# Multiplications and additions on the samples' states scheduled ahead of other work in a hybrid decoder step

## The chip, the cores and the metric

The kernel runs on one core of a Trainium2 chip. The metric is the device time of one execution in microseconds. Its engines are TensorE (matrix products; PE in the profile, PEld its loads of weights), VectorE (DVE), ScalarE (ACT), GpSimd (POOL) and SyncE (SP), which only issues DMAs here. Each engine works through its own list of instructions in a fixed order, and waits on semaphores for the others.

## What is computed

One step of a one-layer decoder trunk, for a prompt of 256 tokens and for 8 samples with 8 new tokens each (320 tokens in all, model width 2048). Cut to what matters:

```python
h = rms_norm(x)
u, v, z, xBC, dt = split(h @ W_in)            # 2048, 2048, 2048, 3072 and 32 columns
xBC = silu(causal_depthwise_conv(xBC))        # 4 taps
y, state = ssd_scan(x, dt, a, B, C, state)    # 32 heads of 64, 4 groups, state of 128
mix = concat(chunk_mlp(u, v), rms_norm(y * silu(z)))
x = x + rms_norm(mix @ W_out)
x = x + rms_norm(conv_ffn(rms_norm(x)))       # 2048 -> 2 x 5632 -> 2048
```

The scan has for each sample and head a state of 64 x 128 numbers that comes in and goes out. Over the 8 new tokens of a sample it becomes

```python
new_state = state * exp(total decay) + sum over tokens of (decayed x) * B
```

The change is about this line for the samples: the multiplication, and the addition of the sum.

## The kernel before

**Products.** All matrices are in float32. `slab` (L109 to L126) loads 128 x 1024 weights with SyncE (`wraw`, L115), makes their high part on ScalarE (`whi`, L118) and their low part on VectorE (`wlo`, L120). `accumulate` (L127 to L131) makes three matmuls of a product: high by high (L129), high by low (L130), low by high (L131). There are three buffers of each kind. A load is issued when its buffer comes free; SyncE's list is in a fixed order, so what is behind a load that waits also waits.

**Stages.** `project` computes columns of W_in slab by slab, `chunk_out` computes four row blocks of W_out and adds each result to a sum in SBUF (L217, VectorE). The groups of the scan are computed beside them: `ssd(g)` is a generator, and after each slab `tick` runs it to its next `yield`. So the scan's instructions are issued between the large products, for groups 0 to 3 in the order of this list:

```python
chunk_out(w_out, 3, ...); heads_out(0); heads_in_next(2)
chunk_out(w_out, 4, ...); heads_out(1); heads_in_next(3)
chunk_out(w_out, 5, ...); heads_out(2); heads_out(3)
```

`heads_in` projects x, B and C for a group, with the convolution on VectorE (`cv`, L388, three per block), ScalarE and GpSimd (small copies L378, L379, L390, L391). `heads_out` projects z, multiplies the scan's result with silu(z) (L963), sums squares (ScalarE L281, VectorE L282, TensorE's `tsum` L263) for the norm.

**A group's states.** The 8 samples are taken in four pairs i = 0 to 3, with two tiles `st` of 128 x 512 each, six buffers in all. SyncE loads them (L743), TensorE multiplies them with C (`yo_ps`, L817), ScalarE picks the samples' B (`bm`, L822), and GpSimd multiplies them by the decay in `shrunk` (L825 to L828, the operation is recorded at L827). A step later `grown` (L830 to L835) makes two matmuls `up_ps` (L833) and adds them to the tiles with VectorE (L834). ScalarE then issues the stores (L839). `up_ps` takes its PSUM bank from the pool `ms`, of four banks, that most small products of the kernel share (`misc`); a bank is given back when its reader has run. State loads of the next pairs or groups wait for stores to land, since they use the same six buffers.

**The scan's products.** For each two heads SyncE loads sums of decays (`cs`, L750), VectorE (L895) and ScalarE (L888, L897) make their exponentials, VectorE masks them (L899), TensorE multiplies (`y_ps`, L910). `yo_to_xdt` (L845) puts the product with the old states beside x.

**The order of the work.** A scheduler orders each engine's list when the program is compiled. What is issued inside `tc.high_priority(offset=...)` is taken ahead of other work that is ready; `first()` is this with an offset of 200000, and slabs use 100000. Additions of `chunk_out` (L217), the reading of the convolution's input and what belongs to a norm are inside `first()` already; the convolution (L388) is not.

Of the kernel before, what the change touches and what calls it, by code (L numbers as in the profile page):

```python
# [13 lines left out]
ALU = mybir.AluOpType  # L14
# [3 lines left out]
P = 128  # L18
# [16 lines left out]
def hybrid_step(  # L35
# [10 lines left out]
    act, dve, pool, pe, sp = nc.scalar, nc.vector, nc.gpsimd, nc.tensor, nc.sync  # L46
# [10 lines left out]
    def misc(name):  # L57
        return ms.tile([P, 512], F32, tag="ms", name=name)
# [6 lines left out]
    with tc.high_priority(offset=300000):  # L65
        dve.memset(ones, 1.0)

        ps = misc("early")
# [35 lines left out]
    def first():  # L104

        return tc.high_priority(offset=200000)
# [151 lines left out]
    def token_sums(*sqs):  # L258

        ps = misc("tsum")  # L260
        for c, o in enumerate((0, P, NT - P)):
            for i, sq in enumerate(sqs):
                ins = pe.matmul(ps[:, c:c + 1], sq[:, o:o + P], ones[:, 0:1], start=i == 0, stop=i == len(sqs) - 1).ins  # L263
        sums_ins.append(ins)
        return ps[:, 0:3]
# [98 lines left out]
    with ExitStack() as mctx:  # L364
        op = mctx.enter_context(tc.tile_pool(name="op", bufs=1))
# [43 lines left out]
        tote = op.tile([P, NH, NB], F32, name="tote")  # L409
# [296 lines left out]
        with tc.tile_pool(name="sd", bufs=1) as sd:  # L706
# [7 lines left out]
            for c in range(4):  # L714
                ps = misc("bt_ps")
# [11 lines left out]
            def by_head(ap):  # L727
                return ap.rearrange("p (h d) -> p h d", d=64)
# [4 lines left out]
            def ssd(g):  # L733

                xs = x_of[g]
                h0 = 8 * g
# [25 lines left out]
                for c in range(4):  # L762
                    ps = misc("xt_ps")
# [6 lines left out]
                    i = c - 2  # L770
# [7 lines left out]
                ps = misc("cb_ps")  # L778
# [3 lines left out]
                for r in range(2):  # L782
# [3 lines left out]
                                  in0=ps[:, :NP].rearrange("p (c t) -> p c t", c=2),  # L786
                                  in1=upper.unsqueeze(1).to_broadcast([P, 2, P]), op=ALU.mult)
# [11 lines left out]
                for hb in range(2):  # L799
                    dve.tensor_tensor(out=cms[:, 4 * hb:4 * hb + 4], in0=cmask[:, 4 * hb:4 * hb + 4],  # L800
                                      in1=cT[:, g, NP + 32 * hb:NP + 32 * hb + 32].unsqueeze(1).to_broadcast([P, 4, 32]),
                                      op=ALU.mult)
                yield

                ps = misc("s1_ps")
# [17 lines left out]
                    return bm  # L823

                def shrunk(i, st):  # L825
                    for h in range(2):
                        pool.tensor_tensor(out=by_head(st[h]), in0=by_head(st[h]),  # L827
                                           in1=tote[:, h0:h0 + 8, 4 * h + i:4 * h + i + 1].to_broadcast([P, 8, 64]), op=ALU.mult)  # L828

                def grown(st, bm):  # L830
                    for h in range(2):
                        ps = misc("up_ps")
                        made = pe.matmul(ps, bm[:, h], xsp[:, h], start=True, stop=True)  # L833
                        dve.tensor_tensor(out=st[h], in0=st[h], in1=ps, op=ALU.add)  # L834
                    return made.ins  # L835

                def store_state(i, st, by=act):
# [12 lines left out]
                def begin(i):  # L850
                    with_c(i, sts[i])
                    bms[i] = picked(i)
                    shrunk(i, sts[i])

                def end(i, by=act):
                    made = grown(sts[i], bms.pop(i))
                    store_state(i, sts[i], by)
                    return made
# [63 lines left out]
                for j in range(5):  # L922
                    for i in range(2):
                        if j < 4:
                            decays(2 * j + i)
                        if j and i == 0:
# [5 lines left out]
                                   in1=dec[:, 2, h0:h0 + 8].unsqueeze(2).to_broadcast([P, 8, 64]), op=ALU.mult)  # L932
# [78 lines left out]
            with first():  # L1011
# [4 lines left out]
                with tc.issue_after(sums_ins[-1]):  # L1016
                    ps = token_sums(*one)
# [37 lines left out]
    with tc.tile_pool(name="fp", bufs=1) as fp:  # L1055
# [113 lines left out]
        with tc.issue_after(made):  # L1169
            ps = token_sums(*one)  # L1170
# [109 lines left out]
```

## Time and profile before

| | |
|---|---|
| median of 3 runs | 1798.79 us (1796.71 to 1799.12) |
| profiled execution, whole | 1800.87 us |
| its span | 1799.2 us |
| VectorE's work from 460 to 560 us | 86.02 of 100 us |
| VectorE's work from 560 to 650 us | 77.55 of 90 us |
| TensorE's work from 560 to 650 us | 88.94 of 90 us |
| additions to states (L834) | 32, 0.68 us each |
| multiplications of states (L827) | 32, 1.05 to 2.62 us each, median 1.22 |

The span runs from the first to the last instruction of the trace; the profiled execution's own time is 1.67 us longer. In a row of the timeline stand the start, the duration, the engine, the line, the operation, the tiles and their shapes and, in brackets, how long the engine stood idle before it and who ended that. SPq and ACTq are DMAs issued by SyncE and ScalarE. In a row of the windows view stand the stretch, its length, then the busy time of TensorE, its weight loads, VectorE, ScalarE and GpSimd with the number of instructions, TensorE's granted clock as a share of full speed, the DMA share and GB/s.

### The profile page before, as it was taken

What the parts mean: (1) busy time and instruction counts of PE and PEld (TensorE: products, weight loads), DVE (VectorE), ACT (ScalarE), POOL (GpSimd) and SP (SyncE); (2) the same over time, 40 slices, a digit from 0 to 9 for tenths busy, and PEclk for the clock granted to TensorE, in tenths of its full rate; (3) what the DMA queues carried; (4) which work ended last, traced back from release to release, by engine and by line L of the source; (5) the groups of instructions that cost most, each with busy time, mean ns of one, the idle gap of its engine ahead of it and who ended that gap; (6) DMA issues with size and microseconds to landing.
All of it is one profiled execution on the core that took longest, in us unless ns stands there. A gap on an engine that the chain in (4) does not pass through costs nothing.

```text
span 1799.2 us, 31167 instructions
## 1 busy us (share of the span) xinstructions
PE 1776.3 (99%) x12200; PEld 1741.7 (97%) x12200; DVE 1190.1 (66%) x2048; ACT 795.4 (44%) x1105; POOL 295.4 (16%) x619
## 2 busy tenths in 40 slices
PE   9999999999999999999999999999999999999998
PEld 8999999999889899999999999999999999999997
DVE  5458664556987969776875474747566565656575
ACT  6444454334545446445554433333434343433335
POOL 3102200000431313104331010111101020101004
PEclk9999999999999999999999999999999999999999
DMA  8646544455566574654554555455545554454542
GB/s 276 194 141 195 159 143 152 153 153 177 180 193 192 167 234 147 178 169 146 174 149 151 155 152 151 148 154 153 153 145 154 152 156 145 153 152 153 151 150 102
DMA packets 222226, 292.56 MB, mean 163 GB/s; under 512 B 16672, under 2 KB 150656, under 8 KB 221888
## 3 DMA queue, kind: packets, MB, share of 16 engines
q1 hardware_dynamic: 209392, 268.12, 49.3%
q10 hardware_dynamic: 10304, 14.82, 2.3%
q0 software_dynamic: 2384, 7.64, 1.4%
q8 instruction: 96, 1.57, 0.4%
q14 instruction: 50, 0.41, 0.1%
HBM read 275.71 MB, written 14.82 MB: 161 GB/s over the span
## 4 chain that ended last, share of the span: by engine, by line
PE 92%; DVE 4%; DMA 2%; issue 1%; ACT 1%; POOL 0%; ACTq 0%; DVEq 0%; POOLq 0%
PE ps L129 20%; PE ps L131 19%; PE ps L130 19%; PE pd L129 10%; PE pd L131 10%; PE pd L130 10%; DMA wraw<-in_w_in 1%; DVE wlo L120 1%; PE y_ps L910 1%; PE yo_ps L817 0%; PE up_ps L833 0%; PE sg L670 0%; ACT whi L118 0%; PE tsum L263 0%; PE vt_ps L582 0%
## 5 line engine op out<-in xcount | busy, mean ns | idle before, releaser
L120 DVE TENSOR_TENSOR wlo<-wraw,whi 128x1024 fp32r<-128x1024 f32 (+1 forms) x474 | 587.6, 1240 | 440.0 <-ACT whi L118 438.2
L118 ACT CAST whi<-wraw 128x1024 fp32r<-128x1024 f32 (+1 forms) x475 | 494.7, 1042 | 717.1 <-PE ps L130 414.8
L129 PE MATMUL ps<-h_hi,whi 128*128 128x320 f32 x2524 | 783.5, 311 | 4.0 <-ACT h_hi L346 2.1
L131 PE MATMUL ps<-h_hi,wlo 128*128 128x320 f32 x2524 | 781.4, 310 | 2.1 <-DVE wlo L120 1.9
L130 PE MATMUL ps<-h_lo,whi 128*128 128x320 f32 x2524 | 780.8, 309 | 0.0
L129 PEld LDWEIGHTS ps<-h_hi,whi 128*128 128x128 f32 x2524 | 475.6, 189 | 7.9 <-issue 2.7
L131 PEld LDWEIGHTS ps<-h_hi,wlo 128*128 128x128 f32 x2524 | 475.4, 188 | 4.1 <-DVE wlo L120 3.5
L130 PEld LDWEIGHTS ps<-h_lo,whi 128*128 128x128 f32 x2524 | 475.6, 188 | 0.7 <-DVE h_lo L546 0.2
L129 PE MATMUL pd<-fhi,whi 128*128 128x320 f32 x704 | 217.2, 309 | 0.0
L131 PE MATMUL pd<-fhi,wlo 128*128 128x320 f32 x704 | 217.2, 309 | 0.0
L130 PE MATMUL pd<-flo,whi 128*128 128x320 f32 x704 | 217.2, 308 | 0.0
L129 PE MATMUL pd<-ohi,whi 128*128 128x320 f32 x448 | 139.6, 312 | 0.0
L131 PE MATMUL pd<-ohi,wlo 128*128 128x320 f32 x448 | 138.4, 309 | 0.0
L130 PE MATMUL pd<-olo,whi 128*128 128x320 f32 x448 | 138.3, 309 | 0.0
L130 PEld LDWEIGHTS pd<-flo,whi 128*128 128x128 f32 x704 | 132.2, 188 | 0.0
L129 PEld LDWEIGHTS pd<-fhi,whi 128*128 128x128 f32 x704 | 132.2, 188 | 0.0
L131 PEld LDWEIGHTS pd<-fhi,wlo 128*128 128x128 f32 x704 | 132.2, 188 | 0.0
L1091 POOL COPY ptf<-pad 128x2 f32<-128x2 f32 x88 | 21.0, 238 | 621.1 <-DVE pad L1079 620.4
L217 DVE TENSOR_TENSOR acc_ffn<-acc_ffn,pd 128x320 f32<-128x320 f32 x160 | 77.6, 485 | 37.9 <-PE pd L131 36.4
L129 PEld LDWEIGHTS pd<-ohi,whi 128*128 128x128 f32 x448 | 84.1, 188 | 1.4 <-issue 0.6
L131 PEld LDWEIGHTS pd<-ohi,wlo 128*128 128x128 f32 x448 | 84.1, 188 | 0.5 <-issue 0.4
L130 PEld LDWEIGHTS pd<-olo,whi 128*128 128x128 f32 x448 | 84.2, 188 | 0.2
(301 smaller groups left out, 1592.3 us busy)
## 6 DMA issues: line engine op xcount, KB each, us to landing
wraw<-in_ffn_w_up SPq DMA_DIRECT2D x176, 512.0 KB, 3.7
wraw<-in_w_in SPq DMA_DIRECT2D x144, 512.0 KB, 3.7
wraw<-in_ffn_w_down SPq DMA_DIRECT2D x88, 512.0 KB, 3.5
wraw<-in_w_out SPq DMA_DIRECT2D x64, 512.0 KB, 3.5
st<-in_state_ssm SPq DMA_DIRECT2D x32, 256.0 KB, 4.5
out_ssm_state_sample<-st ACTq DMA_DIRECT2D x30, 256.0 KB, 4.6
cs<-dacs_d SPq DMA_DIRECT2D x16, 320.0 KB, 4.3
xr<-in_xT SPq DMA_DIRECT2D x4, 640.0 KB, 4.0
```

The costliest lines, as they stand in the source:

```text
L118: act.copy(hi[:, o], raw[:, o])
L120: dve.tensor_tensor(out=lo[:, :m], in0=raw[:, :m], in1=hi[:, :m].bitcast(F32), op=ALU.subtract)
L129: pe.matmul(ps, whi, xhi, start=first, stop=False)
L130: pe.matmul(ps, whi, xlo, start=False, stop=False)
L131: return pe.matmul(ps, wlo, xhi, start=False, stop=last).ins
L217: dve.tensor_tensor(out=acc[:, nb, :], in0=acc[:, nb, :], in1=ps[:, :NT], op=ALU.add)
L910: pe.matmul(ps[64 * i:64 * i + 64, cols], w(hl), x(hl, m, cpx), tile_position=(0, 64 * i), **flags)
L1091: pool.tensor_copy(ptf[:, k, :], pad[:, 256:258])
```

## The change

The two multiplications of a pair of samples on GpSimd, and each addition on VectorE, are issued inside `first()`. The matmuls, the loads and the stores are issued as they were.

```diff
                 def shrunk(i, st):
-                    for h in range(2):
-                        pool.tensor_tensor(out=by_head(st[h]), in0=by_head(st[h]),
-                                           in1=tote[:, h0:h0 + 8, 4 * h + i:4 * h + i + 1].to_broadcast([P, 8, 64]), op=ALU.mult)
+                    with first():
+                        for h in range(2):
+                            pool.tensor_tensor(out=by_head(st[h]), in0=by_head(st[h]),
+                                               in1=tote[:, h0:h0 + 8, 4 * h + i:4 * h + i + 1].to_broadcast([P, 8, 64]), op=ALU.mult)
 
                 def grown(st, bm):
                     for h in range(2):
                         ps = misc("up_ps")
                         made = pe.matmul(ps, bm[:, h], xsp[:, h], start=True, stop=True)
-                        dve.tensor_tensor(out=st[h], in0=st[h], in1=ps, op=ALU.add)
+                        with first():
+                            dve.tensor_tensor(out=st[h], in0=st[h], in1=ps, op=ALU.add)
                     return made.ins
```

The scheduler then gives these instructions, and some around them, other places in the lists of VectorE, GpSimd, ScalarE and SyncE. In TensorE's list only two things move: in group 0 the second `up_ps` of a pair stands right behind the first instead of four matmuls later, and the `tsum` of group 1's norm stands 13 matmuls earlier. In group 1 ScalarE's list has two more loads of its function table. Lines behind the change are two higher in the changed kernel (`grown`'s addition is L836, L899 is L901).

## The prediction, made before the run

> **What bounds the kernel now.** I read the engines' busy time on the page first.
>
> ```profile
> span 1799.2 us, 31167 instructions
> PE 1776.3 (99%) x12200; PEld 1741.7 (97%) x12200; DVE 1190.1 (66%) x2048; ACT 795.4 (44%) x1105; POOL 295.4 (16%) x619
> ```
>
> TensorE works for 1776.3 of 1799.2 us. The change takes nothing off TensorE, so it can only win where TensorE stands still. The waits of TensorE come next (total, times, longest).
>
> ```profile
> PE up_ps L833 <- DVE st L834: 2.8, 1, 2.8
> ...
> PE ps L131 <- DVE wlo L120: 1.9, 3, 0.7
> ...
> PE tsum L263 <- DVE ssq L282: 1.1, 1, 1.1
> ...
> PE y_ps L910 <- DVE cs L899: 0.7, 2, 0.4
> ```
>
> One wait, 2.8 us, is for the very addition that is moved. The waits for low parts of weights (wlo) are three, none over 0.7: low parts mostly come in time, which is the cover for VectorE work put ahead of them. The profiled execution took 1800.87 us (span 1799.2 and 1.67 around it), 2.08 above the median of the runs, 1798.79. I work in differences from it and take them off the median. About 0.2% (3.6 us) is what a measurement of this kernel can tell from no change.
>
> **The change part by part.** It adds no multiplication, addition, matmul or DMA: the same 32 additions and 32 multiplications get another place, and ScalarE loads its table two times more (below). In the order of the compiled program the two additions of a state now stand together as soon as their matmuls can be there, ahead of low parts and convolutions. Five places matter or might.
>
> *Group 0, 475 to 485 us.* TensorE, then VectorE, then GpSimd in the timeline:
>
> ```profile
> 479.77 0.31 PE L129 MATMUL pd<-ohi,whi 128*128 128x320 f32 x1
> 482.86 0.50 PE L833 MATMUL up_ps<-xsp,bm 128*128 128x512 f32 x1 [2.77 <-DVE st L834]
> ```
>
> ```profile
> 477.04 0.48 DVE L217 TENSOR_TENSOR acc_mix<-acc_mix,pd 128x320 f32<-128x320 f32 x1
> 477.43 0.57 DVE L388 SCALAR_TENSOR_TENSOR cv<-pad,prm,cv 128x344 f32<-128x344 f32 x1
> ...
> 482.13 0.67 DVE L834 TENSOR_TENSOR st<-st,up_ps 128x512 f32<-128x512 f32 x1
> ```
>
> ```profile
> 459.87 2.50 POOL L827 TENSOR_TENSOR st<-st,tote 128x512 f32<-128x512 f32 x2 [2.10 <-PE yo_ps L817]
> ```
>
> The matmul at 482.86 needs a PSUM bank that the addition at 482.13 gives back. That addition's state was ready at 462.4 (459.87 + 2.50). It only stood in line behind convolutions and a low part. In the changed order both additions follow the sum at 477.04: they start near 477.43 and 478.03 (0.60 apart), and the bank is free before 479. The wait goes. Matmuls follow each other by 0.15 (12 from 653.43 to 655.19, quoted below), so the slot was 479.92, and TensorE regains 482.86 − 479.92 = **2.94**. The low parts behind the additions slip by 1.2, which the cover above takes; without it up to 1.2 would be lost.
>
> What is late next is the scan's product y_ps of head pair 2, with SyncE's queue, VectorE and TensorE:
>
> ```profile
> 490.52 5.03 SPq L743 DMA_DIRECT2D st<-in_state_ssm  x3
> 495.60 0.43 SPq L115 DMA_DIRECT2D wraw<-in_w_in  x1
> 496.12 0.44 SPq L750 DMA_DIRECT2D cs<-dacs_d  x1
> ```
>
> ```profile
> 501.95 0.29 DVE L895 TENSOR_SCALAR cs<-cs,nda 128x128 f32<-128x128 f32 x1 [2.80 <-DMA cs<-dacs_d]
> 502.15 0.48 DVE L899 TENSOR_TENSOR cs<-cs,cb_cms 128x320 f32<-128x320 f32 x1
> ```
>
> ```profile
> 503.76 0.66 PE L910 MATMUL y_ps<-cs,xdt 128*64 128x128 f32 x8
> ```
>
> The load of cs is issued at 496.12, behind state loads, and VectorE gets it 5.83 later. With TensorE 2.94 earlier, y_ps wants L899 done by 500.82 instead of 503.76; it ended at 502.63. State loads (L743) wait for the stores of the additions that now come earlier, and I place the issue of cs near 494.15, behind a weight load that waits for its buffer: L899 then ends near 500.7. Just in time. I give back 0.1 (bounds 0 and 1.8) and count **−2.8**.
>
> *Group 1, 577 to 600 us.* Here VectorE is the later engine. TensorE, VectorE, GpSimd, ScalarE, SyncE:
>
> ```profile
> 597.40 0.43 PE L910 MATMUL y_ps<-cs,xdt 128*64 128x128 f32 x2 [0.31 <-DVE cs L899]
> 598.20 0.54 PE L910 MATMUL y_ps<-cs,xdt 128*64 128x128 f32 x5 [0.37 <-DVE cs L899]
> ```
>
> ```profile
> 580.23 1.40 DVE L388 SCALAR_TENSOR_TENSOR cv<-pad,prm,cv 128x344 f32<-128x344 f32 x1
> ...
> 589.57 0.68 DVE L834 TENSOR_TENSOR st<-st,up_ps 128x512 f32<-128x512 f32 x1
> ...
> 591.30 0.68 DVE L834 TENSOR_TENSOR st<-st,up_ps 128x512 f32<-128x512 f32 x1
> ...
> 594.56 0.45 DVE L895 TENSOR_SCALAR cs<-cs,nda 128x128 f32<-128x128 f32 x2 [0.93 <-DMA cs<-dacs_d]
> ```
>
> ```profile
> 580.20 1.06 POOL L827 TENSOR_TENSOR st<-st,tote 128x512 f32<-128x512 f32 x1 [2.25 <-PE yo_ps L817]
> ...
> 581.66 2.04 POOL L827 TENSOR_TENSOR st<-st,tote 128x512 f32<-128x512 f32 x1
> ```
>
> ```profile
> 589.29 1.28 ACT L888 ACT_TABLE_LOAD   x1
> 590.28 0.34 ACTq L839 DMA_DIRECT2D out_ssm_state_sample<-st  x1
> ```
>
> ```profile
> 588.76 0.37 SPq L750 DMA_DIRECT2D cs<-dacs_d  x1
> ...
> 595.29 2.27 SPq L743 DMA_DIRECT2D st<-in_state_ssm  x2
> ```
>
> ```profile
> DMA to landing us min/median/max: 2.0/4.4/6.7
> ```
>
> (The last row is of the state stores, L839.) The additions move from 589.57 and 591.30 to right behind the convolution at 580.23, that is to 581.6. The second needs GpSimd's second multiplication, which now follows the first directly: it ends at 581.26 + 1.06 = 582.3 if it runs like the first, at 583.3 if it takes 2.04. VectorE therefore waits 0.1 to 1.1; I take 0.5, since the first price was had beside the same convolution. The Trainium skill, "SBUF — State Buffer", section "SBUF: two separate sides", says that a GpSimd operation and a VectorE operation with two SBUF inputs lock each other out for a whole instruction. By that rule a VectorE that stands waiting leaves GpSimd its 1.06, and the wait is the 0.1; by the row of 2.04 it is 1.1, a difference of 1.0 on VectorE.
>
> Queued behind the waiting addition are a low part, two convolutions and the product xdt; TensorE's waits above name none of them at this place, so they have time to spare. The price comes by SyncE. The stores of these states move from 590.28 to about 583.1 and 583.7. The next two state loads, which wait for them to land, now stand ahead of the weight slab and of the cs load instead of at 595.29. With a median landing of 4.4 to 4.6 they go at 588.3, the slab and cs by 589.3 instead of 588.76, so VectorE resumes near 595.1 instead of 594.56. The two waits of TensorE, 0.31 and 0.37, grow by that; with ScalarE's two extra table loads (1.28 each, in idle time) I take **+0.7**. Bounds: −0.7, if both waits go, and +1.6, if the stores land a microsecond later.
>
> *Starts of groups 1, 2 and 3.* Additions of a pair stand together instead of around a low part, which slips 0.6. Covered: **0**, at worst 0.6.
>
> *Group 1's normalisation, 650 to 657 us.* TensorE, VectorE and ScalarE:
>
> ```profile
> 653.43 0.31 PE L129 MATMUL ps<-h_hi,whi 128*128 128x320 f32 x1
> ...
> 655.19 0.31 PE L129 MATMUL ps<-h_hi,whi 128*128 128x320 f32 x1
> 656.63 0.83 PE L263 MATMUL tsum<-ones,ssq 128*128 128x1 f32 x6 [1.14 <-DVE ssq L282]
> ```
>
> ```profile
> 652.15 0.49 DVE L963 TENSOR_TENSOR xs<-xs,zs 128x320 f32<-128x320 f32 x1
> 654.95 1.23 DVE L120 TENSOR_TENSOR wlo<-wraw,whi 128x1024 fp32r<-128x1024 f32 x1 [2.31 <-ACT whi L118]
> ```
>
> ```profile
> 653.87 1.05 ACT L118 CAST whi<-wraw 128x1024 fp32r<-128x1024 f32 x1 [2.67 <-DMA wraw<-in_w_in]
> 654.82 0.47 ACT L281 ACTIVATE sq<-xs 128x320 f32<-128x320 f32 x1
> ```
>
> Before, the last square and its sum stand behind a weight slab that arrives late. The planner now puts them ahead of it, and tsum 13 matmuls earlier: its slot moves from 655.19 + 0.15 = 655.34 to 653.43. The sum is done at 652.64 + 0.47 + 0.48 = 653.6, nearly in time. Of the 1.29 lost so far (656.63 − 655.34) about 0.3 stays: **−1.0** (bounds −1.3 and −0.5).
>
> Sum: −2.8 + 0.7 + 0 − 1.0 = **−3.1**. The profiled execution would come to 1797.8, the median to 1798.79 − 3.1 = **1795.7**, 0.17% faster.
>
> **The rivals.** (a) *Group 1 costs nothing*: the stores land as fast as their fastest (2.0), SyncE isn't held, and only −2.8 and −1.0 stay: 1795.0; with the two waits gone as well, 1794.3. For it speaks that the cs load needs only half a microsecond; against it that VectorE has no other idle time there. (b) *The stall also cost clock in some runs.* The windows view (TensorE busy after the length, PEclk after POOL):
>
> ```profile
> 478.46:481.87 3.41, 1.62 (x11) 1.32 (x9) 3.41 (x5) 0.34 (x2) 2.92 (x3) 1.00 0.60 207
> ...
> 847.10:850.52 3.42, 2.12 (x8) 2.12 (x9) 3.42 (x7) 2.42 (x6) 1.15 (x2) 0.50 0.20 77
> ```
>
> Here the stall left half a window busy and the clock stayed 1.00; at 847.10 thinner work brought 0.50. If the 2.8 us lie wholly in one window, 0.6 of it is busy, and half clock for one window costs 1.7: 1795.7 − 1.7 = 1794.0. The Trainium skill, "TensorE: Matmul & The Clock Gate", Part 1, has windows of 3413 ns that run free of the kernel, and half rate after an idle one; by that rule the price falls in some executions only, and the trace at hand shows one without it. (c) *The stall moves on*: cs comes no earlier in group 0, y_ps waits until 502.63 and 1.8 of the 2.94 is given back: 1798.79 − 1.1 + 0.7 − 1.0 = 1797.4. For it: cs waits behind three state loads. That the change doesn't touch the stall at all I hold for excluded: the addition is named as the releaser and moves 4.7 us. (d) *Slower*: in group 1 SyncE, held for the stores to land, delays the slab and cs. Past 589, each microsecond goes one for one into the two waits for L899. From 592.5 on it eats all gains, from 596 it costs over 3.6 more (1802.5). That needs stores issued 5 us later than I have them, by ScalarE behind a cast, as cs at 588.76 came behind a slab; against it, the longest landing is 6.7.
>
> **How the numbers follow.** My forecast (1795.2 to 1797, within 0.2%) 0.39; (a) 0.26 and (b) 0.14, faster by over 0.2%; (c) 0.09, within; (d) 0.12, slower. So faster 0.40, within 0.2% 0.48, slower 0.12. The range leaves out (d). It goes down to (b) with the first and the last step at their lower bounds (1794.0 − 0.14 − 0.3), 1793.5, and up to (c) with group 1 at its upper bound (1797.4 + 0.9), 1798.3.
>
> **What would show it.** The wait of up_ps for st is gone and the matmul follows within 0.2 us; tsum waits under 0.4; y_ps waits for L899 about 1.3 in all, near 595 to 600; TensorE's busy time as before. A new wait of over 1 us on y_ps near 500 shows (c); state loads ahead of cs at 590 or later show (d). It is wrong if any other wait of TensorE grows by over 1 us, in groups 2 and 3 above all, where I priced nothing.

## The result and the profile after

Twelve timed executions of the changed kernel have a median of 1793.45 us (1790.35 to 1797.33), twelve of the kernel before 1798.95 (1795.86 to 1805.07). The ratio is 0.9969, 95% interval 0.9958 to 0.9980: 5.6 us faster, 0.31%. I had forecast 1795.7, within 0.2%, with the range from 1793.5 up: the gain is larger than I had it, and the time lies just outside.

The profiled execution of the changed kernel took 1796.18 us, 4.69 less than the one before. First the page:

```profile
span 1794.3 us, 31172 instructions
PE 1774.6 (99%) x12200; PEld 1741.1 (97%) x12200; DVE 1185.2 (66%) x2048; ACT 797.8 (44%) x1107; POOL 293.2 (16%) x619
```

TensorE has the same 12200 matmuls, but they took 1.7 us less. The prediction held that this number would stay; it's the first hint that not only waits changed. Now the waits of TensorE:

```profile
PE x1p L1164 <- DVE acc_ffn L1190: 2.4, 2, 2.1
...
PE ps L129 <- DVE acc_mix L217: 0.9, 1, 0.9
...
PE y_ps L912 <- DVE cs L901: 0.8, 1, 0.8
```

The wait of up_ps for st (2.8) and that of tsum for ssq (1.1) are gone. The wait of y_ps for cs is 0.8 where it was 0.7. A wait of 0.9 for acc_mix is new. In group 0, TensorE and then VectorE:

```profile
477.48 0.62 PE L834 MATMUL up_ps<-xsp,bm 128*128 128x512 f32 x2
477.95 0.31 PE L129 MATMUL pd<-ohi,whi 128*128 128x320 f32 x1
```

```profile
474.80 0.48 DVE L217 TENSOR_TENSOR acc_mix<-acc_mix,pd 128x320 f32<-128x320 f32 x1
475.20 1.27 DVE L836 TENSOR_TENSOR st<-st,up_ps 128x512 f32<-128x512 f32 x2
476.39 1.97 DVE L120 TENSOR_TENSOR wlo<-wraw,whi 128x1024 fp32r<-128x1024 f32 x1
```

Both additions stand behind the sum of acc_mix, as forecast, and both matmuls run with no bracket behind them. At group 1's norm, VectorE and TensorE:

```profile
648.28 0.49 DVE L965 TENSOR_TENSOR xs<-xs,zs 128x320 f32<-128x320 f32 x1
649.37 0.49 DVE L282 TENSOR_TENSOR ssq<-ssq,sq 128x320 f32<-128x320 f32 x1 [0.60 <-ACT sq L281]
```

```profile
649.96 0.78 PE L263 MATMUL tsum<-ones,ssq 128*128 128x1 f32 x6
```

The sum of squares now waits only for its square, 0.60, and tsum for nothing.

To see where time went, I took the start of the same matmul of TensorE's list in both traces. At the places named by the times of before, the changed execution is ahead by:

| at (us of before) | 235 | 260 | 472 | 500 | 530 | 580 | 640 | 670 | 900 |
|---|---|---|---|---|---|---|---|---|---|
| ahead by (us) | 0.14 | 1.68 | 1.62 | 4.65 | 3.75 | 3.75 | 3.47 | 4.82 | 4.83 |

Between 235 and 260 nothing of the change can act; 1.54 us come from there all the same. There before ran one window of 3.4 us at half clock, this execution none. From 472 on the terms of the prediction stand one after the other: 3.03 in group 0, 0.90 given back at 508, 0.28 given back in group 1, 1.35 at the norm. Their sum is 3.20, and the prediction had 3.1. That agreement is partly luck: the terms differ from the forecast ones, and the 0.90 will turn out to be no part of the change. So one pair of profiles agrees with the forecast, and the times say 5.6. The experiments had to tell what the pair doesn't show.

**Two theories.** *Waits*: what repeats is the 3.1 of the waits, the rest is spread between executions. *Clock*: the stall of group 0 also puts TensorE to half clock in some executions (the prediction's rival b), and the rest of the gain is that.

### The profile page after: what moved, and what is told of

Its sections match the earlier page's. It is cut to its first block, busy times and chain, and to the rows that moved or that the text cites. A ratio compares the mean times of both kernels' runs of the same rounds, so it can differ in the third digit from the quotient of the medians.

```text
span 1794.3 us, 31172 instructions
## 1 busy us (share of the span) xinstructions
PE 1774.6 (99%) x12200; PEld 1741.1 (97%) x12200; DVE 1185.2 (66%) x2048; ACT 797.8 (44%) x1107; POOL 293.2 (16%) x619
## 4 chain that ended last, share of the span: by engine, by line
PE 91%; DVE 4%; DMA 3%; issue 1%; ACT 1%; POOL 0%; DVEq 0%; ACTq 0%; POOLq 0%
PE ps L129 20%; PE ps L131 19%; PE ps L130 19%; PE pd L129 9%; PE pd L131 9%; PE pd L130 9%; DMA wraw<-in_w_in 1%; DVE wlo L120 1%; DMA cs<-dacs_d 1%; PE y_ps L912 1%; PE yo_ps L817 0%; PE sg L670 0%; DVE cv L388 0%; PE up_ps L834 0%; DVE cs L897 0%
```

## The experiments

**e1: the kernel before again.** No edit.

> The kernel before, unchanged. Waits theory (the whole gain is the waits that TensorE lost or won in the profiled pair, -2.06 in group 0, +0.28 in group 1, -1.37 at the normalisation, together -3.1 us, and the rest of the 5.5 us between the medians is spread between executions): same time within 0.1%, and a mean granted clock of its executions like that of the changed kernel's twelve, 0.9969. Clock theory (the 2.8 us stall of group 0 sets TensorE to half clock in some executions, which costs 1.7 us per window of 3.4 us, and the remaining 2.4 us of the gain are that): a mean granted clock near 0.9955, 1.4 windows more per execution.

Measured: ratio 1.0004 (0.9992 to 1.0016), so two sets of executions are told apart to about 0.1%. Its mean granted clock over 11 executions is 0.9953, over 35 of before beside it 0.9957. With e5's they are 69 in all: mean time 1798.9 us (standard error 0.3), mean clock 0.9955. The number is the one the clock theory wanted; what it is worth comes below.

**e2, e3, e4: one group alone.**

```diff
-                    with first():
+                    with first() if g == 0 else nullcontext():
```

in both functions, and `g == 1` and `g == 2` likewise.

> first() in group 0 alone. Waits theory: no wait of up_ps for st, the 0.9 us wait of the next projection for acc_mix is there, tsum still waits 1.1 us; -2.1 us (0.9988). Clock theory: -4.5 us (0.9975), and a mean granted clock of its executions near 0.9969.

> first() in group 1 alone; TensorE's order is that of before. Both theories: the wait for st of group 0 stays; waits of y_ps for cs grow by 0.3 us, time 0 to +0.7 us (1.0000 to 1.0004); the granted clock like that of the kernel before.

> first() in group 2 alone, which moves tsum of group 1's norm ahead. Both theories: the wait for st of group 0 stays, the wait of tsum is gone, -1.4 us (0.9992); the granted clock like that of the kernel before.

| | ratio | 95% interval | waits of TensorE for st, tsum, y_ps |
|---|---|---|---|
| e2, group 0 | 0.9981 | 0.9968 to 0.9995 | gone, not listed, 0.8 |
| e3, group 1 | 0.9992 | 0.9981 to 1.0004 | 2.8, not listed, not listed |
| e4, group 2 | 0.9998 | 0.9987 to 1.0010 | 2.8, not listed, 1.3 |

"Not listed" is less than 0.3. Group 0 brings the only clear gain, 3.4 us, between the two theories' numbers; its clock (0.9958) didn't rise. Several expectations missed: in e2 the 0.9 for acc_mix didn't come and tsum waited 0.2 instead of 1.1, in e3 the wait of y_ps went away instead of growing, and e4's 1.4 us aren't seen in its times. The trace of e4 shows the clock theory's mechanism in one execution. TensorE, then the windows view laid on the clock's windows (length, TensorE busy, ..., PEclk after POOL's):

```profile
481.19 0.50 PE L834 MATMUL up_ps<-xsp,bm 128*128 128x512 f32 x1 [2.77 <-DVE st L836]
```

```profile
478.02:481.43 3.41, 0.64 (x4) 0.37 (x3) 3.41 (x6) 1.35 (x3) 2.09 (x4) 1.00 0.48 154
481.43:484.84 3.41, 3.41 (x14) 3.37 (x14) 2.75 (x6) 0.68 (x3) 0.00 (x0) 0.53 0.33 112
```

The stall is the same 2.77 as before, but here all of it lies in one window of the clock (478.19 to 481.61; the view's stretches lie 0.2 earlier), in which TensorE is busy for 0.64 us. The next window is granted half clock: 14 matmuls where a full one has some 25. e4 lost 1.53 us there. In the profile of before the stall was cut by a window's end into 1.81 and 0.97, and the clock stayed.

**e5: the changed kernel again.** No edit.

> The changed kernel, unchanged. Waits theory: the gain that repeats is the -3.1 us of the waits, so the ratio comes back nearer to 0.9983, and a mean granted clock between 0.9957 (46 executions of before) and 0.9969 (the first twelve of the changed kernel). Clock theory: 0.9970 again, and a mean granted clock near 0.9969.

Measured: 1793.78 us, ratio 0.9974 (0.9965 to 0.9984), mean clock 0.9970. The larger gain repeats. Over both sets, 24 executions, the mean is 1793.7 (standard error 0.4), 5.2 below the 69 of before, with an error of 0.5. With the 21 other executions of before on record, those beside the first result and beside e9, before has a mean of 1799.2, which makes the gain 5.5.

**e6: the additions alone.** `shrunk` as before, `grown` as changed.

> Only the additions in first(). Every engine's order is that of the changed kernel but for one place of GpSimd: in group 1 the two small copies for the convolution's input stand between the two multiplications, as before. Both theories: the same time as the changed kernel within 0.1%; the clock like the changed kernel's; VectorE's second addition of that pair waits 0.5 us longer for GpSimd.

Measured: 1794.36 us, ratio 0.9977 (0.9965 to 0.9989), the same as the changed kernel within their intervals. GpSimd's part moves nothing but this in group 1 (GpSimd, VectorE):

```profile
574.14 1.06 POOL L828 TENSOR_TENSOR st<-st,tote 128x512 f32<-128x512 f32 x1 [2.25 <-PE yo_ps L817]
575.14 0.10 POOL L378 MEMSET pad<- 128x3 f32 x1
575.18 0.46 POOL L379 COPY pad<-sst 128x24 f32<-128x24 f32 x1
575.59 1.06 POOL L828 TENSOR_TENSOR st<-st,tote 128x512 f32<-128x512 f32 x1
```

```profile
576.68 0.69 DVE L836 TENSOR_TENSOR st<-st,up_ps 128x512 f32<-128x512 f32 x1 [0.52 <-POOL st L828]
```

VectorE waits 0.52 here, and 0.36 in the changed kernel. The gain is that of the additions.

**e7, e8: what a stall costs.** Twenty stalls are put into the steady products of the feed-forward part of the kernel before. TensorE makes a tiny matmul with a tile `x` of its own, GpSimd multiplies that tile, and a second tiny matmul waits for it; the next slab's matmuls are held behind that. The edit, cut:

```diff
+    def stall():
...
+        with first(), tc.issue_after(last_mm[0]):
+            made = pe.matmul(ps[:, 0:1], ones, x[:, 0:1], start=True, stop=True).ins
+        with first():
+            for _ in range(2):
+                pool.tensor_tensor(out=x, in0=x, in1=x, op=ALU.mult)
+        with first(), tc.issue_after(made):
+            return pe.matmul(ps[:, 1:2], ones, x[:, 0:1], start=True, stop=True).ins
...
+            held_by = stall() if stalls and i == 3 else None
```

e8 has one multiplication per stall.

> The kernel before with 20 stalls of TensorE put into the up-projections of the feed-forward part: TensorE waits there for two multiplications of GpSimd on a tile of its own (2.1 us at 1.05 each, 4 us at 2.0 each, plus handing over). The result does not depend on them. Clock theory: some of the 20 are followed by half clock for one window of 3.4 us, about one in four at 2.8 us and more at 3.5 us, each costing up to 1.7 us on top of its wait; the mean granted clock falls by 0.001 per window. Waits theory: the clock stays 1.00 after all of them, and the time grows by the waits alone.

> As the long stalls, with one multiplication of GpSimd each (1.05 to 2.0 us, plus handing over). Clock theory: none or few of the 20 stalls are followed by half clock, since TensorE stays busy for half of every window of 3.4 us. Waits theory: none.

Waits of TensorE, e7 and e8:

```profile
PE stall_ps L164 <- POOL late L162: 62.8, 20, 3.4
```

```profile
PE stall_ps L164 <- POOL late L162: 23.6, 20, 1.2
```

e8 took 1834.88 us with a mean clock of 0.9962: 36 us for 23.6 us of waits and the 40 tiny matmuls, and no stall was followed by half clock. e7 took 1910.35 with 0.9735: 112 us for 62.8 us of waits. In its trace 19 of the 20 stalls are followed by half clock; the first, the shortest (2.7), isn't. That is far more often than I expected at this length.

**e9, e10: the length of the real stall, idle and filled.** e9 cuts the second multiplication to 344 of 512 columns. e10 adds to e9, between the two tiny matmuls, products that nobody reads:

```diff
+        for _ in range(18):
+            with first(), tc.issue_after(made):
+                made = pe.matmul(ps[:, 8:8 + NT], hT[0][:, 0, :P], hT[0][:, 0, :], start=True, stop=True).ins
```

> The 20 stalls of the feed-forward part with a second multiplication cut to 344 of 512 columns, so that TensorE stands idle about 2.5 us with two tiny matmuls around it: about the wait of group 0, 2.77. From the traces so far (windows of 3.41 us in which TensorE stood idle for up to 1.9 us kept full clock, one with 2.8 us lost it; long stalls 19 of 20): clock theory 8 to 15 of the 20 are followed by half clock, a mean granted clock of 0.983 to 0.989, and 13 to 25 us over the waits. Waits theory: clock 0.9955, and 20 times the wait and its handing over, about 60 us.

> As the mid stalls, and in each of them TensorE makes 18 useless matmuls of 128x320 instead of standing idle (2.65 us); the next slab still begins when GpSimd is done. Clock theory: the clock stays at 0.9955 and the time is 13 to 25 us below that of the mid stalls. Waits theory: the same time as the mid stalls.

Measured: 1903.65 and 1866.32 us (means 1902.6 and 1866.4), mean clocks 0.9735 and 0.9964. One stall of e9, and then the windows view of the whole part, of e9 and of e10 (TensorE alone: busy, PEclk):

```profile
1293.86 0.28 PE L159 MATMUL stall_ps<-late,ones 128*128 128x1 f32 x2
1297.01 0.38 PE L164 MATMUL stall_ps<-late,ones 128*128 128x1 f32 x2 [2.88 <-POOL late L162]
...
1298.53 0.47 PE L131 MATMUL ps<-h_hi,wlo 128*128 128x320 f32 x1
1298.79 0.47 PE L129 MATMUL ps<-h_hi,whi 128*128 128x320 f32 x1
...
1301.22 0.31 PE L130 MATMUL ps<-h_lo,whi 128*128 128x320 f32 x1
1301.37 0.31 PE L131 MATMUL ps<-h_hi,wlo 128*128 128x320 f32 x1
```

```profile
910.00:1820.00 910.00, 852.77 (x5563) 0.95 0.45 134
```

```profile
910.00:1800.00 890.00, 887.31 (x6036) 1.00 0.46 140
```

Matmuls follow each other by 0.26 behind the stall and by 0.15 from 1301 on. With the same stalls filled, the clock stays 1.00 and 36 us are saved: 1.8 us per stall on average, over and above its wait, come from the clock. The time between the two tiny matmuls is the same in both, 3.1 to 3.4 us in all stalls but the first (2.7 and 2.9). The clock theory's bound (25) was too low, since I had counted one window for each of 15 stalls; 19 of 20 lost the clock, seven of them for two windows.

**e11: the change without group 1.**

```diff
+                    with first() if g != 1 else nullcontext():
```

> The changed kernel with first() in groups 0, 2 and 3 only. By the prediction's step (+0.7 us in group 1): 0.7 us faster than the changed kernel. By the profiles after it (-0.4 to -0.8 us in group 1 in five of six changed executions): 0.4 to 0.8 us slower, about 1794.5; in the profile a wait of y_ps for cs of 0.7 us or more. A difference of this size is near the noise of the times, so the profile's waits count.

Measured: 1792.83 us (five executions, mean 1792.8, standard error 0.3), ratio 0.9953 (0.9940 to 0.9966); the changed kernel's 24 have a mean of 1793.7. The profile shows no wait of y_ps for cs at all. So my reading of the profiles was wrong: the wait at 597 comes and goes without a change in group 1. That this version beats the changed one, by 0.9 with an error of 0.5, is likely at most. (Against the nine executions of before beside it, whose mean is 1800.9, it is 8.1 ahead, so the comparison by ratio points the same way.)

**All profiles together.** Where TensorE gains (−) or loses against the profiled execution of before, by stretches of its time; nothing but the named stretches differs by over 0.3 from 260 to 900 us. The last column is the time from issue to landing of the one load of cs that VectorE waits for near 594, which took 5.8 us before:

| execution | 235–260 | 472–500 | 500–530 | 580–640 | 640–670 | cs landing |
|---|---|---|---|---|---|---|
| e1, before again | −0.04 | +0.04 | +0.19 | +0.84 | −0.16 | 6.6 |
| e3, group 1 | −0.02 | −0.01 | +0.17 | −0.79 | −0.82 | 4.2 |
| e4, group 2 | +1.52 | +1.53 | +1.00 | +0.59 | −1.35 | 6.4 |
| e7 | −1.54 | 0 | −0.13 | −1.19 | −0.75 | 4.5 |
| e8 | −0.02 | 0 | +0.60 | +0.65 | −1.25 | 6.4 |
| e9 | −1.54 | −0.01 | −0.21 | +0.23 | −0.78 | 6.0 |
| e10 | −1.54 | −0.01 | +0.15 | −1.22 | −0.69 | 4.5 |
| e2, group 0 | −1.54 | −3.03 | −0.28 | +0.08 | −0.95 | 5.9 |
| changed | −1.54 | −3.03 | +0.90 | +0.27 | −1.35 | 5.5 |
| e5, changed again | −1.52 | −3.03 | +0.13 | −0.91 | −1.35 | 4.8 |
| e6, additions | −0.04 | −3.03 | −0.19 | −0.59 | −1.34 | 4.4 |
| e11, without group 1 | −1.55 | −3.01 | +0.70 | −1.20 | −1.35 | 4.6 |

In the first stretch all kernels have the same instructions, and a half-clock window comes or not. The five executions with group 0's part gain 0.84 more there than the eight without (error 0.5), which I count as chance, since nothing of the change acts there. It is about as large as what stays open at the end. The other columns, mean of those with that part of the change less mean of those without (before itself is 0): group 0 −3.03 less 0.19, of which the 0.19 is e4's clock, one execution in eight; 500–530 no difference (0.25 and 0.22); 580–640 −0.51 less −0.14; the norm −1.35 less −0.68. The sum is −3.22 + 0.03 − 0.37 − 0.67 = −4.2 us. The spread between profiles gives this sum an error of about 0.5, of which group 1's stretch has 0.4. The times say −5.2 with an error of 0.5, or −4.8 with e6's among the changed ones.

The stretch 580–640 follows the landing of that load of cs. The DMA view of it, in e1 and in e10 (the last number is the time to landing):

```profile
cs<-dacs_d SPq DMA_DIRECT2D x1, 320.0 KB, 6.6
cs<-dacs_d SPq DMA_DIRECT2D x1, 320.0 KB, 4.5
```

In all nine executions without group 1's part SyncE issues it at the same place, 588.76 in TensorE's time of before, and the slower it lands, the later y_ps comes. Where it lands within 4.8 us, y_ps waits for nothing: the three such executions with group 1's part then gain 0.59 to 0.91, the three without it 1.19 to 1.22. And the changed execution (5.5) loses 0.27 where e2 with a slower landing (5.9) loses 0.08. So at an equal landing group 1's part seems to cost 0.3 to 0.6, as e11's time suggests too, and its −0.37 comes from landings that were on average 0.9 shorter. Whether the change shortens them or they fell so isn't shown; e7, e10 and e11 have them as short without it.

## Why the prediction was wrong, by its own steps

- **What bounds the kernel, and where the change can win**: right. Each gain lies where TensorE stood still.
- **Group 0, −2.94 and 0.1 given back**: right in mechanism and size. The stall goes in every execution with that part, for 3.03. y_ps was in time; the 0.90 given back in one changed execution, in a wait for acc_mix, is no part of the change, since the stretch differs as much among the unchanged ones.
- **Group 1, +0.7**: this step failed. The waiting of VectorE was right (0.36, from bounds 0.1 and 1.1, with GpSimd's second multiplication at the lower price), the price by SyncE was not. SyncE in the changed kernel:

```profile
581.15 0.93 SPq L743 DMA_DIRECT2D st<-in_state_ssm  x2
583.60 0.38 SPq L115 DMA_DIRECT2D wraw<-in_w_out  x1
585.21 0.38 SPq L750 DMA_DIRECT2D cs<-dacs_d  x1
```

I let the state loads wait until the stores had landed after a median 4.4 to 4.6 us, and had the cs load at 589.3 instead of 588.76. The first state load went at 581.15, 2.6 after the first store's issue at 578.52: these stores landed in 2.0 us, the lower of the two ends of 2.0 to 6.7. The load of cs went at 585.21, which is 3.55 earlier than before where TensorE was 3.75 ahead: 0.2 late (0.2 to 0.35 in the four traces with this part), not the half microsecond that I had. What sets the wait of y_ps is how long that load takes to land, 4.2 to 6.6 us in the thirteen profiles, and I had held it at the 5.8 of the one at hand. The stretch came out at −0.4 with an error of 0.4 in place of +0.7. That it can win isn't shown: at equal landings it seems to cost, by 0.3 to 0.6.
- **The norm, −1.0**: the step was right (−1.35 against the profiled execution). The average gain is 0.7, since the wait of 1.14 that I priced was the longest of all profiles of that order; the others lost 0.16 to 1.25 less.
- **The clock (rival b)**: right in kind, and I gave it 0.14 and left it out of the sum. It is part of the stall's price: 1.53 us where the stall falls into one window (e4), 1.8 us per stall of this length in a steady stage (e9 against e10). By the Trainium skill, "TensorE: Matmul & The Clock Gate", Part 1, half rate follows an idle window. In e4 a window with 0.64 us of work was enough. In how many timed executions the stall of before did it isn't shown: in eight profiles it was one. An estimate: 1.89 us of the stall in one window kept the clock (e7) and 2.77 lost it, so if the windows fall anywhere, the stall pays in 0.19 to 0.70 of the executions, 0.3 to 1.1 us on average at 1.53 each. Against the upper end speaks e2, whose clock is that of before. The row at 847.10, which I read as thin work that brought 0.50, is itself the window at half clock; the one ahead of it had TensorE busy for 2.28 of 3.42 us.
- **The stores that hold SyncE (rival d), the stall that moves on (c)**: neither came.

So the failed step is group 1's +0.7: SyncE was hardly held, the landing of cs was not fixed, and −0.4 stands in its place. With the other terms as measured (group 0 −3.0 and 0.2 of clock, the norm −0.7) the sum is −4.2 instead of −3.1. The remaining 0.6 to 1.3 us between that and the times is within two standard errors. It stays open, and so does why the changed kernel's executions have a mean clock of 0.9970 and those of before 0.9955. The mean clock is no measure of the stall: the half-clock windows per profile with and without group 0's part are 0.2 and 0.75 near 240 us, 1.2 and 1.75 near 847, and 0 and 0.125 at the stall, so nearly all of the difference lies away from the change. Part of that clock costs nothing: the half-clock windows at 847 to 854, of which there are one or two per execution, change TensorE's lead from 670 to 900 us by under 0.3 (the most is e7, the others under 0.1).

## What to carry to other kernels

An engine that is the bound waits little, so read each of its waits, and find what the releaser stood behind: here an addition whose inputs had been ready stood for four microseconds behind work with time to spare. Take several profiles before a wait of a microsecond is priced: those that hang on a DMA's landing or on a tight order came out between 0 and 1.5 us from one execution to the next, and the one at hand need not be the mean. Compare two kernels at such a place only at an equal landing. A stall of TensorE of some 2.8 us should be priced with the clock that it may cost: 1.5 us more in the one profile that showed it here, 1.8 on average in the steady stage.

## What the runs showed of the hardware

- Stalls of 1.2 us in steady products never cost the clock (20 of 20), stalls of 2.9 us with a tiny matmul on either side 19 times of 20; the half clock then lasted one window of 3.41 us, or two. In the real stall, windows with 1.4 to 1.9 us of idle time kept full clock in seven profiles, and one with 2.77 lost it. In e7 and e9 the windows that cost the clock had 1.72 to 2.88 us without a matmul, those that kept it at most 1.73. So the idle time within one window tells more than the stall's length, but it doesn't settle the matter alone: 1.72 lost the clock in e7 where 1.89 kept it in the real stall, and near 847 us a window busy for 2.28 us was followed by half clock.
- The same load of 320 KB, issued at the same place of TensorE's work in nine executions, took 4.5 to 6.6 us to land, and the stage behind it moved by 2.1 us with it.
- The stage around 240 us, of the same instructions in every kernel, had no half-clock window in seven profiles, one in five and two in one: about 1.5 us each that no change made.
